# Two more early tiles of one gate, and the early gates loaded by another queue

## The chip, the core and the metric

The kernel runs on one core of a Trainium2 chip. The metric is the device time of one execution in microseconds (us), the lower the better. Three runs of the kernel before took 2232.28 to 2233.12 us, with a median of 2232.4. Engines are named as the profile names them: PE is TensorE (matmul), DVE is VectorE, ACT is ScalarE, POOL is GpSimd, SP is SyncE, which here only issues DMAs.

## What is computed

One step of a decoder layer for 1024 prompt tokens and 64 sample tokens together (1088 columns). Four token mixers (0: stick-breaking attention, 1: gated convolution, 2: RWKV-7, 3: spatial gating) each give a branch of 256 channels. What the change touches is their gated sum:

```
proj  = einsum('nlic,icd->nlid', br, w_branch)          # four branches, each 256 -> 1024
gates = sigmoid(x @ w_gate + b_gate).reshape(n, L, 4, 1024)
mix   = sum_i gates[i] * proj[i]
x     = LN1(alpha * x + mix @ w_o)                        # then memory cross-attention, then the MLP
```

Each gate i is 8 tiles of 128 channels by 1088 columns. One tile's gate is a product over 1024 inputs, its projection one over 256.

## The kernel before

All matrices are kept as a high and a low part of a 32-bit format, and each product is three matmuls (high by high, high by low, low by high). The 1088 columns are cut into three pieces of 384, 384 and 320, so a piece of a gate tile is 8 x 3 = 24 matmuls (tile `mm`) and a piece of its projection 2 x 3 = 6 (tile `pp`). A weight tile comes into a raw buffer `wraw`, ACT casts its high part `whi`, DVE subtracts the low part `wlo`; the projection's weights go the same way (`pwr`, `pwh`, `pwl`), a branch too (`braw`, `bhi`, `blo`). All these loads, of gates, projections, branches and of the folded memory weights, share a pool of two raw buffers.

The work runs in stages. First branch 2 (RWKV-7), then branches 3 and 0, which are long chains over all engines. Beside them a list of filler units (`fillers`, `groups`) gives PE matmuls at fixed points of the branches' code: projections of the inputs, branch 1, the memory's keys and values, and the early gates. `EARLY` says which gate tiles are made there: all 8 of gates 1 and 3, and the first tiles of gate 0. An early piece is computed into PSUM, copied by ACT (`gst`, L1268) and written to DRAM (`gate`, L1269, by SP). What is left in the list when branch 0 is done is drained at once (`self.fill(None)`).

Then comes the stage of the gates (`gates`, `add`). `LATE = (2, 0)`: gate 2 is computed here, 8 tiles by 3 pieces, so 24 steps. A step computes one piece of gate 2 and adds up to three pieces of an early gate (gate 1 beside tiles 0 to 3, gate 3 beside tiles 4 to 7), and a unit of the folded memory weights (`fst`, `fmh`). A tile of an early gate is loaded back whole (544 KB) into one of two buffers `add` (L1293, by SP), ACT takes its sigmoid in three pieces (L1311, `add<-add`), DVE multiplies by the projection (L1314) and POOL adds into `mix` (L1316). The piece computed in the step gets its sigmoid by ACT as `sg` (L1311, `sg<-mm`). The projections rotate over three PSUM buffers, so the fourth projection of a step needs DVE to have multiplied the first by `sg`. Last comes gate 0 with the same function: its early tiles are added one piece a step (`more`), tiles 6 and 7 are computed last, and `mix` goes to the output projection.

What order the instructions have on each engine is decided by a scheduler when the program is built, from its own estimate of durations; at run time each engine, and each queue of DMAs, takes its instructions strictly in that order. A DMA waits at its queue's head until its buffer is free, and what stands behind it waits too.

Of the kernel before, what the change touches and what calls it, by code (L numbers as in the profile page):

```python
# [24 lines left out]
CTEMPS = 8  # L25
ABUFS = 4

EARLY, LATE = ((1, 8), (3, 8), (0, 2)), (2, 0)
HALVES = (slice(0, 512), slice(512, 1024))
HR = (slice(0, 64), slice(64, 128))  # L30

# [19 lines left out]
class Kern:  # L51
# [1229 lines left out]
    def gates(self, w3):  # L1281
        nc, I = self.nc, self.I
        br, mix, begun = {}, {}, set()
        w0, br[LATE[0]] = self.first
        br[EARLY[0][0]] = self.load_br(self.bp[1], EARLY[0][0])
        ready = dict(EARLY)

        def add(i, m):

            early = m < ready.get(i, 0)  # L1290
            if early:
                gm = self.sp.tile([128, T], F32, name="add", tag="add", bufs=2)
                nc.sync.dma_start(gm, self.early[i][m])  # L1293
            else:
                w = w0 if i == LATE[0] and m == 0 else self.split_w(I["w_gate"][8 * i + m])
            p = self.branch_w(i, m)
            bh, bl = br[i]
            if m not in mix:
                mix[m] = self.g("mix", [128, T], self.xp)
            part = lambda a, kt: tuple(x[:, kt * 128:kt * 128 + 128] for x in a)  # L1300
            for c, (c0, n) in enumerate(CH):
                cs = slice(c0, c0 + n)
                if early:
                    src = sg = gm[:, cs]
                else:
                    ps = self.mm_ps()
                    self.gemm_b(ps, n, lambda kt: part(w, kt), lambda kt: (self.xhi[c][:, kt, :n], self.xlo[c][:, kt, :n]))
                    src, sg = ps[:, :n], self.sp.tile([128, 384], F32, name="sg", tag="sg", bufs=3)[:, :n]
                pp = self.wk_ps("pp")
                self.gemm_b(pp, n, lambda kt: part(p, kt), lambda kt: (bh[kt][:, cs], bl[kt][:, cs]), kts=2)  # L1310
                nc.scalar.activation(sg, src, AF.Sigmoid, bias=self.vec[:, 8 * i + m:8 * i + m + 1])  # L1311
                first = (m, c) not in begun
                begun.add((m, c))
                nc.vector.tensor_mul(mix[m][:, cs] if first else sg, sg, pp[:, :n])  # L1314
                if not first:
                    nc.gpsimd.tensor_add(mix[m][:, cs], mix[m][:, cs], sg)  # L1316
                yield

        def early(i):
            for m in range(ready.get(i, 0)):  # L1320
                yield from add(i, m)


        folded = self.folded(w3)
        for m in range(8):
            if m % 4 == 0:
                i = EARLY[m // 4][0]
                if m:
                    br[i] = self.load_br(self.bp[1], i)
                more = early(i)  # L1330
            for _ in add(LATE[0], m):
                for _ in range(3):
                    next(more, None)
                next(folded)
            next(folded)
        br[LATE[1]] = self.load_br(self.bp[1], LATE[1])
        more = early(LATE[1])
        for m in range(ready.get(LATE[1], 0), 6):
            for _ in add(LATE[1], m):
                next(more, None)  # L1340
        for _ in more:
            pass

        last = [add(LATE[1], m) for m in (6, 7)]
        act = None
        for c in range(3):
            for a in last:
                next(a)
            act = act or self.new_act()
            if c == 2:  # L1350
                self.wp, self.wi = [w3, w3, *self.wp], -1
                w = [self.split_w(I["w_o"][0, j]) for j in range(4)]
            self.split_mix(mix, act, c)
        return act, w
# [999 lines left out]
```

## Time and profile before

| | us |
|---|---|
| median of three runs | 2232.4 |
| the profiled execution | 2232.75 |
| its span, first to last instruction | 2231.0 |
| PE busy | 2146.9 (96%) |
| DVE busy | 1342.9 (60%) |
| ACT busy | 945.1 (42%) |
| POOL busy | 424.2 (19%) |

The stages on the span's clock: branches with fillers up to about 860 us (the last early gate piece is copied at 867), gate 2 with gates 1 and 3 from 867 to about 1092, gate 0 from there to about 1190, and the rest (output projection, cross-attention, MLP) to 2231. A row of the timeline has a start, a length, an engine, a line, the operation, and in brackets how long the engine was idle before it and what ended that. Matmuls overlap, so how fast they go is read from their starts, not from their lengths. The clock column is the clock that was granted to TensorE, 1.00 for 2.4 GHz.

### The profile page before, as it was taken

The numbers are of one execution on the slowest core, as the hardware profiler recorded it, in microseconds if no ns is written. First come the engines' busy times: TensorE is split into PE (matmuls) and PEld (weight loads), VectorE is DVE, ScalarE is ACT, GpSimd is POOL, SyncE is SP. The second block draws the span as 40 slices with busy tenths as digits, with TensorE's granted clock in tenths as the row PEclk, the third lists the DMA queues.
The fourth block names the chain that finished last, engine by engine and source line by source line (L and its number), as shares of the span: only waits on it lengthen the run. The fifth ranks groups of instructions, "written<-read, shape, count | busy, mean of one in ns | idle before, by whom it ended". The sixth has DMA issues, their size and how long they took to land.

```text
span 2231.0 us, 36111 instructions
## 1 busy us (share of the span) xinstructions
PE 2146.9 (96%) x13674; PEld 1918.4 (86%) x13674; DVE 1342.9 (60%) x2678; ACT 945.1 (42%) x1838; POOL 424.2 (19%) x482
## 2 busy tenths in 40 slices
PE   8998999999999999999999999999999999999998
PEld 8986777888989988998998877778999999788886
DVE  3365778755666674434324673479777776655477
ACT  4343343134555556444322362335444444544341
POOL 0111111012310310123220310000554543100000
PEclk9998999999999999999999999999999999999999
DMA  6322333145543435555324155733776677976552
GB/s 195 105 69 58 100 106 96 43 128 169 163 146 120 132 112 157 173 164 173 108 68 167 71 180 196 255 125 115 248 271 230 235 247 238 318 251 204 163 198 90
DMA packets 184838, 356.11 MB, mean 160 GB/s; under 512 B 36104, under 2 KB 92568, under 8 KB 184664
## 3 DMA queue, kind: packets, MB, share of 16 engines
q1 hardware_dynamic: 174216, 318.24, 43.7%
q0 software_dynamic: 10448, 35.57, 4.7%
q8 instruction: 107, 1.75, 0.3%
q14 instruction: 67, 0.55, 0.1%
HBM read 250.01 MB, written 103.73 MB: 159 GB/s over the span
## 4 chain that ended last, share of the span: by engine, by line
PE 74%; DVE 9%; DMA 9%; ACT 3%; issue 3%; POOL 1%; SPq 1%; DVEq 0%; ACTq 0%; POOLq 0%
PE mm L118 22%; PE m L118 14%; PE dn L2016 13%; PE mm L130 8%; PE sc L130 3%; PE pp L118 3%; DVE tpr L1014 1%; PE ds L2021 1%; PE gr L966 1%; DVE wlo L107 1%; DVE Ti L1015 1%; DMA vp<-in_vpages,pt 1%; DMA Li<-Ld 1%; PE wtp L503 1%; ACT whi L101 1%
## 5 line engine op out<-in xcount | busy, mean ns | idle before, releaser
L118 PE MATMUL mm<-ah,whi 128*128 128x384 f32 (+1 forms) x1176 | 395.8, 337 | 9.2 <-ACT ah L278 4.8
L118 PE MATMUL mm<-al,whi 128*128 128x384 f32 (+1 forms) x1176 | 392.7, 334 | 0.6 <-DVE al L279 0.6
L118 PE MATMUL mm<-ah,wlo 128*128 128x384 f32 (+1 forms) x1176 | 391.9, 333 | 0.6 <-DVE wlo L107 0.6
L2016 PE MATMUL dn<-dop 128*128 128x512 f32 x1344 | 317.9, 391 | 2.9 <-ACT dop L1691 2.9
L2016 PEld LDWEIGHTS dn<-dop 128*128 128x128 f32 x1344 | 253.0, 188 | 57.8 <-ACT dop L1691 3.3
L107 DVE TENSOR_TENSOR wlo<-wraw,whi 128x1024 fp32r<-128x1024 f32 (+2 forms) x145 | 158.9, 1104 | 173.0 <-ACT whi L101 170.1
L118 PEld LDWEIGHTS mm<-ah,whi 128*128 128x128 f32 x1176 | 224.5, 191 | 18.8 <-ACT ah L278 5.4
L118 PEld LDWEIGHTS mm<-al,whi 128*128 128x128 f32 x1176 | 224.3, 191 | 6.7 <-issue 3.5
L101 ACT CAST whi<-wraw 128x1024 fp32r<-128x1024 f32 (+1 forms) x130 | 132.9, 1027 | 228.3 <-PE mm L118 100.5
L118 PEld LDWEIGHTS mm<-ah,wlo 128*128 128x128 f32 x1176 | 224.3, 191 | 4.2 <-issue 1.9
L1692 DVE TENSOR_TENSOR dop<-wraw,dop 128x512 fp32r<-128x512 f32 x224 | 152.7, 713 | 109.2 <-ACT dop L1691 108.5
L118 PE MATMUL m<-xht,wo 128*128 128x272 f32 x1024 | 201.4, 292 | 5.3 <-DVE u L1894 3.2
L1691 ACT CAST dop<-wraw 128x512 fp32r<-128x512 f32 x224 | 133.0, 620 | 152.3 <-PE dn L2016 80.4
L130 PE MATMUL mm<-wlo,ah 128*128 128x512 f32 (+1 forms) x488 | 168.4, 349 | 3.7 <-DVE wlo L107 3.7
L130 PE MATMUL mm<-whi,ah 128*128 128x512 f32 (+1 forms) x488 | 169.1, 348 | 1.0 <-ACT stA L301 0.5
L118 PEld LDWEIGHTS m<-xht,wo 128*128 128x128 f32 x1024 | 164.8, 191 | 5.7 <-ACT u L1720 3.4
L130 PE MATMUL mm<-whi,al 128*128 128x512 f32 (+1 forms) x448 | 155.1, 346 | 0.0
L118 PE MATMUL m<-xh,wo 128*128 128x272 f32 x768 | 153.1, 293 | 0.0
L118 PE MATMUL m<-xlt,wo 128*128 128x272 f32 x512 | 149.1, 291 | 0.0
L118 PEld LDWEIGHTS m<-xh,wo 128*128 128x128 f32 x768 | 124.4, 191 | 0.0
L118 PE MATMUL m<-xl,wo 128*128 128x272 f32 x384 | 111.7, 291 | 0.0
L130 PEld LDWEIGHTS mm<-wlo,ah 128*128 128x128 f32 x488 | 92.4, 190 | 17.9 <-DVE wlo L107 4.8
(509 smaller groups left out, 4215.6 us busy)
## 6 DMA issues: line engine op xcount, KB each, us to landing
wraw<-hs SPq DMA_DIRECT2D x112, 256.0 KB, 4.1
wraw<-in_w_up SPq DMA_DIRECT2D x36, 512.0 KB, 4.6
wraw<-in_w_gate SPq DMA_DIRECT2D x32, 512.0 KB, 3.6
dw<-in_w_down SPq DMA_DIRECT2D x32, 512.0 KB, 4.9
hs<-sh SPq DMA_DIRECT2D x64, 256.0 KB, 2.6
wt<-dw SPq DMA_DIRECT2D x32, 512.0 KB, 3.4
wraw<-wt SPq DMA_DIRECT2D x64, 256.0 KB, 4.5
wraw<-in_w_down SPq DMA_DIRECT2D x48, 256.0 KB, 4.9
```

The lines of the kernel that those rows point to most:

```text
L101: nc.scalar.copy(hi[:, c], raw[:, c])
L107: nc.vector.tensor_sub(lo[:, c], raw[:, c], hi[:, c].bitcast(F32))
L118: nc.tensor.matmul(ps[:, :n], a, b, start=first and i == 0, stop=last and i == len(steps) - 1, skip_group_check=not first)
L130: nc.tensor.matmul(ps[:, :n], a, b, start=i == 0, stop=i == len(steps) - 1)
L503: self.nc.tensor.transpose(ps[:b.shape[-1], j * 128:j * 128 + 128], b, self.ident)
L966: nc.tensor.matmul(g[hh][:nb, j, :nb], p[HR[hh], pr, cs], q[HR[hh], pr, cs], start=True, stop=True)
L1014: nc.vector.tensor_mul(tv, Ti[:, 0:h, 0:t + 1], Li[:, 0:t + 1, t:t + 1].rearrange("p s o -> p o s").to_broadcast([128, h, t + 1]))
L1015: nc.vector.tensor_reduce(Ti[:, 0:h, t:t + 1], tv, axis=AX.X, op=ALU.add)
L1691: nc.scalar.copy(o[:, 0], src)
L1692: nc.vector.tensor_sub(o[:, 1], src, o[:, 0].bitcast(F32))
L2016: nc.tensor.matmul(ps[j], hs[:, a, c], w[:, b], start=first and k == 0, stop=last and k == 2, skip_group_check=n >= 16 and steps[n][0] in ...
L2021: nc.tensor.matmul(sp, rows[p][:, smp[i]].rearrange("p a n -> p (a n)"), ops[n][1][:, b], start=i != 2 and p == 0 and b == 0, stop=p == 15 ...
```

## The change

Three edits. `EARLY` gives gate 0 four early tiles, not two: six more pieces (24 matmuls each, a copy `gst`, a write to DRAM) join the end of the filler list, and their 144 matmuls leave the stage of gate 0. The load of every early tile (18 before, 20 now) is issued by POOL's queue, which has POOL's own instructions between, and no longer by SP's. And in the stage of gate 0, where now two tiles (4 and 5) and not four are computed before the last pair, two early pieces are added in each of six steps, not one in each of the first six of twelve.

```
-EARLY, LATE = ((1, 8), (3, 8), (0, 2)), (2, 0)
+EARLY, LATE = ((1, 8), (3, 8), (0, 4)), (2, 0)
...
             if early:
                 gm = self.sp.tile([128, T], F32, name="add", tag="add", bufs=2)
-                nc.sync.dma_start(gm, self.early[i][m])
+                nc.gpsimd.dma_start(gm, self.early[i][m])
...
         more = early(LATE[1])
         for m in range(ready.get(LATE[1], 0), 6):
             for _ in add(LATE[1], m):
                 next(more, None)
+                next(more, None)
```

The scheduler puts other rows around this. On PE the order is the same up to the end of branch 0 and in the stage of gate 2, and changes at the tail of branch 0 and in the stage of gate 0. On ACT it changes in the stage of gate 2 too.

ACT at the tail of branch 0, from the first sigmoid of an early gate. `e` and `z` are the attention's chain (L347 exponential, L348 logarithm, L355 exponential), whose two last `z` PE waits for; an ACT_TABLE_LOAD stands ahead of a function of another set. Before:

```order
L1268 COPY gst<-mm 128x384
L347 ACT_TABLE_LOAD
L347 ACTIVATE e<-e 128x512
L1247 CAST bhi<-braw 128x384
L348 ACT_TABLE_LOAD
L348 ACTIVATE e<-e,eps 128x512
L1247 CAST bhi<-braw 128x384
L1311 ACT_TABLE_LOAD
L1311 ACTIVATE add<-add,vec 128x384
L355 ACT_TABLE_LOAD
L355 ACTIVATE z<-z 128x512 x2
```

The same place now:

```order
L347 ACT_TABLE_LOAD
L347 ACTIVATE e<-e 128x512
L1311 ACT_TABLE_LOAD
L1311 ACTIVATE add<-add,vec 128x384
L355 ACT_TABLE_LOAD
L355 ACTIVATE z<-z 128x512
L348 ACT_TABLE_LOAD
L348 ACTIVATE e<-e,eps 128x512
L1268 COPY gst<-mm 128x320
L101 CAST whi<-wraw 128x1024
L1311 ACT_TABLE_LOAD
L1311 ACTIVATE add<-add,vec 128x320
```

The two casts of a branch and the second logarithm no longer stand ahead of the first of the two `z`. The second `z` comes after one more sigmoid, one more copy `gst` and one more table load, so between the two `z` there now stand a logarithm, two copies, a cast of weights, two sigmoids and three table loads. On PE, which transposes each `z` in four matmuls, 6 matmuls of a filler and not 14 now stand ahead of the first of these transposes, and 34 between the two groups of four, where 5 stood.

ACT in the stage of gate 2, at the first piece of tile 5 (tile 6's first piece has the same two orders). `add` is the sigmoid of the early tile of the next step, `sg` that of the piece which PE needs in this step. Before:

```order
L1233 COPY fst_10414<-mm_10407 128x512
L1219 CAST fmh_10517<-fraw_10515 128x512
L101 CAST whi_10510<-wraw_10509 128x1024
L1311 ACTIVATE add_10567<-add_10567,vec_76 128x384
L1311 ACTIVATE sg_10454<-mm_10429,vec_76 128x384
L1311 ACTIVATE add_10567<-add_10567,vec_76 128x384
L1311 ACTIVATE add_10567<-add_10567,vec_76 128x320
```

The same place now:

```order
L1233 COPY fst_10594<-mm_10587 128x512
L1219 CAST fmh_10697<-fraw_10695 128x512
L101 CAST whi_10690<-wraw_10689 128x1024
L1311 ACTIVATE add_10747<-add_10747,vec_76 128x384 x2
L1311 ACTIVATE add_10747<-add_10747,vec_76 128x320
L1311 ACTIVATE sg_10634<-mm_10609,vec_76 128x384
```

The `sg` stood behind one sigmoid of the loaded tile and stands behind three. In the second pieces of tiles 4 and 5 it stood ahead of all three and stands behind one; in the second piece of tile 6 it stood behind three and stands behind two.

ACT at the start of gate 0, where `whi` is the weight tile after the next. Before:

```order
L1258 CAST pwh<-pwr 128x256
L1311 ACTIVATE sg<-mm,vec 128x320
L1258 CAST pwh<-pwr 128x256
L101 CAST whi<-wraw 128x1024
L1233 COPY fst<-mm 128x512 x2
L1311 ACTIVATE sg<-mm,vec 128x384 x2
```

The same place now:

```order
L1258 CAST pwh<-pwr 128x256
L1233 COPY fst<-mm 128x512
L1311 ACTIVATE sg<-mm,vec 128x320
L1258 CAST pwh<-pwr 128x256
L1233 COPY fst<-mm 128x512 x2
L101 CAST whi<-wraw 128x1024
```

The copies that empty PSUM came behind the cast of a weight tile that has to be loaded first, and now come ahead of it. On POOL each load of an early tile stands right behind the addition that last reads the buffer.

## Rows read from the trace of the kernel before

**Rows 1.** The page, busy time, share of the span and instructions of each engine

```profile
PE 2146.9 (96%) x13674; PEld 1918.4 (86%) x13674; DVE 1342.9 (60%) x2678; ACT 945.1 (42%) x1838; POOL 424.2 (19%) x482
```

**Rows 2.** Windows: start:end, length, busy PE, PEld, DVE, ACT, POOL, clock, DMA, GB/s

```profile
840.00:880.00 40.00, 35.22 (x212) 31.99 (x210) 20.48 (x33) 27.20 (x43) 1.58 (x2) 0.91 0.45 137
...
985.00:1062.00 77.00, 72.57 (x403) 68.31 (x402) 32.79 (x49) 31.46 (x56) 30.89 (x32) 0.98 0.51 158
1062.00:1100.00 38.00, 35.22 (x188) 32.89 (x187) 12.29 (x18) 15.57 (x28) 4.64 (x5) 0.95 0.47 148
```

**Rows 3.** Waits of PE, 838 to 1110 us: total us, times, longest

```profile
PE pp L118 <- DVE sg L1314: 6.7, 6, 2.3
PE wtp L503 <- ACT z L355: 4.0, 1, 4.0
PE mm L118 <- ACT fst L1233: 2.7, 1, 2.7
```

**Rows 4.** Timeline of PE at the tail of branch 0

```profile
848.09 0.34 PE L118 MATMUL mm<-al,whi 128*128 128x384 f32 x1
852.41 1.11 PE L503 MATMUL wtp<-ident,z 128*128 128x128 f32 x4 [3.98 <-ACT z L355]
```

**Rows 5.** Timeline of ACT at the tail of branch 0

```profile
845.55 0.49 ACT L1247 CAST bhi<-braw 128x384 fp32r<-128x384 f32 x1
846.06 1.28 ACT L348 ACT_TABLE_LOAD   x1
847.36 0.72 ACT L348 ACTIVATE e<-e,eps 128x512 f32<-128x512 f32 x1
...
851.73 1.15 ACT L355 ACTIVATE z<-z 128x512 f32<-128x512 f32 x2
```

**Rows 6.** Timeline of PE at the start of gate 0

```profile
1093.47 0.69 PE L118 MATMUL mm<-ah,whi 128*128 128x384 f32 x1 [2.73 <-ACT fst L1233]
1094.27 0.52 PE L118 MATMUL mm<-ah,wlo 128*128 128x384 f32 x1
1094.59 0.52 PE L118 MATMUL mm<-ah,whi 128*128 128x384 f32 x1
```

**Rows 7.** Timeline of ACT at the start of gate 0

```profile
1091.89 1.04 ACT L101 CAST whi<-wraw 128x1024 fp32r<-128x1024 f32 x1 [2.02 <-DMA wraw<-in_w_gate]
1092.84 1.07 ACT L1233 COPY fst<-mm 128x512 f32<-128x512 f32 x2
```

**Rows 8.** The chain in order of time, in the stage of gate 0: start, length, what

```profile
1093.47 5.95 PE mm L118 x24
...
1101.52 4.16 PE mm L118 x24
```

**Rows 9.** Tile `add`, its loads by SP: duration ns min/median/max; landing us

```profile
L1293 SPq DMA_DIRECT2D add<-gate x18: 319/326/422, 833.6 to 1064.0; - x18
...
DMA to landing us min/median/max: 3.6/4.5/6.0
```

**Rows 10.** Tile `vp`, loads of 512 KB by POOL, gathered: ns; landing us

```profile
L507 POOL DMA_INDIRECT vp<-in_vpages,pt x8: 933/948/1777, 544.8 to 802.7; - x8
...
DMA to landing us min/median/max: 4.1/4.7/7.1
```

**Rows 11.** Timeline of POOL and of SP, one release of a buffer `add` and its load

```profile
1025.73 3.02 POOL L1316 TENSOR_TENSOR mix<-mix,add 128x384 f32<-128x384 f32 x3
...
1028.78 0.33 SPq L1293 DMA_DIRECT2D add<-gate  x1
```

**Rows 12.** Timeline of ACT in the stage of gate 2

```profile
992.27 0.58 ACT L1311 ACTIVATE sg<-mm,vec 128x384 f32<-128x384 f32 x1
...
1014.41 0.56 ACT L1311 ACTIVATE sg<-mm,vec 128x384 f32<-128x384 f32 x1
1014.88 1.06 ACT L1311 ACTIVATE add<-add,vec 128x384 f32<-128x384 f32 x2
```

**Rows 13.** Timeline of PE, a late projection in the stage of gate 2

```profile
1058.82 0.41 PE L118 MATMUL pp<-bhi,pwh 128*128 128x320 f32 x1 [2.29 <-DVE sg L1314]
```

More of the change, by code (lines that the diff above doesn't have):

```diff
@@ L26 @@
 ABUFS = 4
-EARLY, LATE = ((1, 8), (3, 8), (0, 2)), (2, 0)
+EARLY, LATE = ((1, 8), (3, 8), (0, 4)), (2, 0)
 HALVES = (slice(0, 512), slice(512, 1024))
@@ L1292, in add @@
                 gm = self.sp.tile([128, T], F32, name="add", tag="add", bufs=2)
-                nc.sync.dma_start(gm, self.early[i][m])
+                nc.gpsimd.dma_start(gm, self.early[i][m])
             else:
@@ L1339, in gates @@
             for _ in add(LATE[1], m):
+                next(more, None)
                 next(more, None)
```

## The prediction

> **What bounds the kernel now.** I read the shares of busy time first: PE is busy for 96% of the span [rows 1], so only what PE waits for, or how fast it is clocked, can move the time. The change leaves PE's count of matmuls alone: the 144 matmuls of two gate tiles go from the stage of gate 0 into the fillers. Then I read the windows around the places that the change touches [rows 2]: PE is idle for about 5 us of 40 at the tail of branch 0, for about 4 of 77 in the second half of gate 2, and for about 3 of 38 where gate 0 begins, and in each the clock's mean is under 1.00. So at most some 12 us and the clock's share are there to be won, on a base of 2232. Third, PE's waits in these stages [rows 3]: six waits for DVE's multiplication by `sg` (6.7 us), one for a `z` of ACT at the tail (4.0), one for a copy `fst` at the start of gate 0 (2.7). Each is priced below. A measurement of this kernel can tell about 0.2% from no change, that is 4.5 us.
>
> **The start of gate 0 (-4.5).** PE stands 2.73 us before the first matmul of this stage, for a PSUM buffer that `fst` empties [rows 6]. ACT was not busy then: it stood 2.02 us at the cast `whi` of a later weight tile, whose load had not landed, with the `fst` copies queued behind it [rows 7]. After the change the `fst` stand ahead of this cast, so the wait for a load is no longer passed on, and the 2.73 us should go. The clock adds to it: behind this wait the matmuls start 0.32 us apart [rows 6], and the 24 of this piece take 5.95 us, where a later 24 take 4.16 [rows 8]. They ran at the 1.2 GHz level after an idle stretch of PE; without it I take the 1.79 us back as well. Sum -2.73 - 1.79 = -4.5. What is late next: the same weight tile's cast, wanted one tile later by PE, with a tile's 3 x 24 matmuls (some 12 us by [rows 8]) as its cover; and the weights of the next early tile's projection, whose load and cast now come twice as fast in a step, since two pieces are added a step. I charge +0.3 for that (bounds 0 and +1.1, one cast of `whi` in [rows 7] whole on the path).
>
> **The tail of branch 0 (-1.0).** PE's last matmul before the wait starts at 848.09, and the transposes of `z` at 852.41 after 3.98 us of waiting [rows 4]. Ahead of that `z` on ACT stood two casts `bhi` (0.49 us the one shown), a table load (1.28) and a logarithm (0.72) [rows 5]: 2 x 0.49 + 1.28 + 0.72 = 2.98 us, which now come later. But PE also has only 6 matmuls of a filler ahead of this wait and not 14; at 4.16 / 24 = 0.173 us each [rows 8] these 8 covered 1.4 us. The first wait becomes 3.98 - 2.98 + 1.4 = 2.4, a gain of 1.6. Against it stands the second `z`: both came as one pair before (1.15 us for two [rows 5]), and now between them ACT has a logarithm (0.72), three table loads (3 x 1.28), a cast of weights (1.04 [rows 7]), two copies and two sigmoids (0.53 each, by the 1.06 for two in [rows 12]) and the `z` itself (0.58): 0.72 + 3.84 + 1.04 + 2.12 + 0.58 = 8.3 us. PE's 34 matmuls between them take 34 x 0.173 = 5.9 us, or 34 x 0.248 = 8.4 at the slower pace of [rows 8]. So a second wait of 0 to 2.4 us; I take 0.6, nearer to the slow end, because PE comes out of the first wait at whatever level that leaves. Sum -1.0, bounds -1.6 and +0.8. The 6 new pieces are matmuls like those around them; their copies and writes go on ACT and SP, which have idle time there (ACT 27 of 40 us busy [rows 2]), and cost nothing as long as nothing of the attention's chain stands behind them.
>
> **ACT's order in the stage of gate 2 (+2.5).** In the first pieces of tiles 5 and 6 the `sg` that PE needs for its fourth projection stands behind three sigmoids of an early tile, where it stood behind one: two more, 1.06 us [rows 12] each time, +2.1. In the second piece of tile 6 one fewer stands ahead: -0.5. In the second pieces of tiles 4 and 5 `sg` stood ahead of all of them (992.27 [rows 12]), and now stands behind one, and so behind the load of that tile; I take +0.5 each, one sigmoid (bounds 0, where the load has landed by then, and +1). Sum 2.1 - 0.5 + 1.0 = 2.6, taken as +2.5. From below the bound is -0.5: the first pieces may have slack for a microsecond, since the trace of before does not show PE waiting in every step (six times in 24 [rows 3]).
>
> **The queue of the loads (+0.8).** On SP an issue took 0.33 us and came right when POOL's last addition had freed the buffer (POOL's three began at 1025.73 and took 3.02, the load was issued at 1028.78) [rows 11]. So SP's queue was not what held these loads; the buffer was, and moving them to POOL's queue, where each stands right behind that addition, wins little at the issue. What can change is how long it takes to land: 4.5 us from SP in the median (3.6 to 6.0) [rows 9]. POOL loading such a tile is not in this trace; the nearest row is POOL's gather of 512 KB, 4.7 us (4.1 to 7.1), with 0.95 us of POOL at the issue [rows 10]. Four of PE's six waits for `sg` stand behind such a load, the longest 2.29 us [rows 13]; so a load that lands later is passed on there in full: 4 x 0.2 = +0.8. Bounds: 4 x (4.1 - 4.5) = -1.6 and 4 x (7.1 - 4.5) = +10.4. POOL's own time for 20 issues, 20 x 0.95 = 19 us, lies beside 424 us of POOL's work in 2231 [rows 1] and in the second half of gate 2 beside 46 idle of 77 us [rows 2]. SP is rid of 18 issues of 0.33 us, and what stood behind them no longer waits for a buffer of `add`: the loads of weights can go out earlier, but only two raw buffers take them, so I give that nothing here.
>
> The Trainium skill bears on this term. Its page "DMA: Bandwidth & Descriptors", section "Specifications", gives the first byte of a DMA about 1 us after issue on the GpSimd path and about 0.6 on that of SP and ACT. By that the term would be an estimate of 4 x 0.4 = +1.6 and the whole sum -1.1, or 2231.3; no run here shows a gate tile loaded by POOL yet, and the gather's row has 0.2 us. Its section "Issuing engines are not separate DMA queues" says that all issuers' DMAs run on the same 16 engines, so that another issuer saves only the time at the sequencer; the 0.33 us of the issue here agree that this is small.
>
> **The sum.** -4.5 + 0.3 - 1.0 + 2.5 + 0.8 = -1.9. The profiled execution took 2232.75 us, its span 2231.0; so 2230.85, and as the median of the runs is 0.35 below it, 2230.5.
>
> **The rivals.** *B, the full gain.* The reordered sigmoids hide in slack and the loads land sooner, because SP's queue no longer mixes them with weights: -4.5 at gate 0, -1.6 at the tail, -0.5 for the one `sg` that moved up, and the four waits behind a load shrink by the gather's best, 4 x (4.5 - 4.1) = 1.6 [rows 9, 10]: -8.2, or 2224.2. For it: the gather's 4.1 us is below 4.5, and SP, too, queues many waiting transfers. Against it: the load waits for the buffer, not for SP [rows 11].
>
> *C, slower.* POOL's loads land late. The place is the stage of gate 2, from tile 4 on, where the load is one step ahead of its use and ACT has `sg` behind it. If the median is 1 us or more above SP's 4.5, about nine steps that have no slack for it (the four that wait already, and the five whose `sg` the new order puts behind a sigmoid of the loaded tile or keeps there) pass on the 1 us each: +9, with -4.5 + 0.3 - 1.0 + 2.5 the sum is +6.3, or 2238.7. It decides for slower from a delay of about 0.8 us (9 x 0.8 - 2.7 = +4.5). For it: the gather's longest, 7.1 [rows 10], and a wait that also leaves PE at the lower clock level costs more than its length [rows 8]. Against it: the gather's median.
>
> *D, nothing comes of it.* The wait at the start of gate 0 comes back as a wait of the next tile's matmuls for the cast of the weights whose load was late by 2.02 us [rows 7], the clock falls there as it did, and the other terms cancel: 2232. Against it: 12 us of matmuls as a cover.
>
> **How the numbers follow.** The forecast 0.55, B 0.25, C 0.15, D 0.05. The forecast's own spread, some 2227 to 2235, lies mostly within 4.5 us of 2232.4: faster 0.12, same 0.40, slower 0.03. B is faster for 0.23 and same for 0.02; C slower for 0.13, same for 0.02; D same for 0.04, slower for 0.01. Together faster 0.35, same 0.48, slower 0.17. The range takes in B down to 2223 and C up to 2240 and leaves out what lies beyond either (both queue bounds whole, with the clock).
>
> **What would show it.** Right: PE's first matmul of gate 0 without a wait for `fst`, and its 24 in about 4.2 us; a wait for the first `z` of about 2.4 us and a second below 2.4; the waits for `sg` in the stage of gate 2 at some 8 to 11 us in place of 6.7; landings of `add` at about 4.7. Wrong: landings above 5.3 (C) or near 4.1 with waits for `sg` below 6 (B); a wait of PE for `whi` or `wlo` within the first two tiles of gate 0 (D); a gap of over 2.4 us at the second `z`, or new table loads of ACT on the path of the attention's chain, which would hit the tail's term.

## The result: slower, by the early tiles' loads

The changed kernel took 2246.43 us in the median of four runs (2242.96 to 2249.63), the kernel before 2232.34 beside it: 1.0064 times as long, 95% interval 1.0044 to 1.0085, some 14 us more. The forecast was 2230.5; the result lies above its range and beyond rival C's 2238.7, on C's side. The profiled execution's span was 2247.8 us.

On the page, the line that answers to [rows 1] has hardly changed: the engines do the same work.

```profile
PE 2145.1 (95%) x13674; PEld 1916.2 (85%) x13674; DVE 1341.3 (60%) x2678; ACT 950.2 (42%) x1846; POOL 440.3 (20%) x502
```

PE's waits in the stages that the change touches, 838 to 1130 us (what waited, for what: us in total, times, longest), answer to [rows 3]:

```profile
PE pp L118 <- DVE sg L1314: 24.8, 12, 4.7
PE wtp L503 <- ACT z L355: 2.5, 1, 2.5
PE mm L118 <- ACT sg L1311: 2.0, 2, 1.4
PE yps L447 <- DVE wT L434: 1.3, 1, 1.3
PE pp L118 <- DVE mix L1314: 0.6, 1, 0.6
```

The wait for `fst` at the start of gate 0 (2.7 before) is gone, the first wait for `z` is 2.5 where it was 4.0, and the waits for DVE's multiplication by `sg` went from 6.7 us in six to 24.8 in twelve. The windows (start:end, length, busy PE, PEld, DVE, ACT, POOL, clock, DMA, GB/s), of the tail, the two halves of gate 2, and gate 0, beside [rows 2]:

```profile
840.00:880.00 40.00, 36.17 (x239) 34.49 (x239) 13.74 (x18) 27.18 (x37) 0.55 (x1) 1.00 0.34 112
893.00:1004.00 111.00, 99.08 (x616) 96.86 (x615) 40.78 (x65) 43.81 (x78) 16.31 (x18) 0.97 0.49 153
1004.00:1118.00 114.00, 98.56 (x548) 92.20 (x548) 39.73 (x59) 42.15 (x74) 39.85 (x43) 0.96 0.46 142
1118.00:1215.00 97.00, 96.69 (x565) 93.77 (x564) 45.76 (x74) 38.58 (x75) 29.57 (x29) 1.00 0.35 109
```

The tail now keeps its clock (1.00, before 0.91) and gate 0 waits for next to nothing. All the loss is in the stage of gate 2: PE is idle there for 27 of 225 us and the clock is at 0.97 and 0.96. From the first projection to the last matmul of the folded weights this stage took 219.2 us before and now takes 244.8, 25.6 more. The other two stages got shorter. From the last group of `yps` (branch 0's last products) to the first projection there are 33.0 us, where there were 12.1, but six pieces more of 23.6 in all (twice 4.16 + 4.16 + 3.5) stand in them: 2.7 less. That group itself starts 0.8 later (859.87, before 859.07), which leaves 1.9. Gate 0, from that last matmul to the last projection, took 99.6 and takes 72.7: 26.9 less, of which 23.6 are those pieces, so 3.3 are won. Together -5.2, against +25.6. What comes behind gate 0, which the change does not touch, was 3.6 us shorter in this profile, and with it the sum is 16.8, the difference of the two spans.

One step of gate 2 shows how the loss comes about. The timeline of SP, POOL, ACT, DVE and PE in the changed kernel, gate 1's half; `mqT` is a weight tile of the folded memory weights, of which this step loads two:

```profile
920.05 1.99 SPq L100 DMA_DIRECT2D wraw<-in_w_mqT  x2
921.88 0.56 POOL L1293 DMA_DIRECT2D add<-gate  x1 [2.13 <-issue]
923.59 1.05 ACT L101 CAST whi<-wraw 128x1024 fp32r<-128x1024 f32 x1 [1.53 <-DMA wraw<-in_w_mqT]
...
929.83 1.05 ACT L101 CAST whi<-wraw 128x1024 fp32r<-128x1024 f32 x1 [4.19 <-DMA wraw<-in_w_mqT]
...
930.79 1.57 ACT L1311 ACTIVATE add<-add,vec 128x384 f32<-128x384 f32 x3
...
932.26 0.56 ACT L1311 ACTIVATE sg<-mm,vec 128x384 f32<-128x384 f32 x1
932.85 0.55 DVE L1314 TENSOR_TENSOR sg<-sg,pp 128x384 f32<-128x384 f32 x1 [0.72 <-ACT sg L1311]
...
933.46 0.41 PE L118 MATMUL pp<-bhi,pwh 128*128 128x320 f32 x1 [3.29 <-DVE sg L1314]
```

Both weight tiles and the early tile are in flight at once, the second weight tile reaches ACT at 929.83, some 8 us after its issue, and `sg`, which needs neither, stands behind its cast and behind three sigmoids of an early tile that is added only in the next step (in the kernel before these three stood ahead of that cast). In the other half, with the early tile alone late (POOL's issue, then ACT and PE):

```profile
1095.32 0.56 POOL L1293 DMA_DIRECT2D add<-gate  x1 [0.30 <-POOL mix L1316]
...
1102.25 1.12 ACT L1311 ACTIVATE add<-add,vec 128x384 f32<-128x384 f32 x2 [9.15 <-DMA add<-gate]
1103.28 0.56 ACT L1311 ACTIVATE sg<-mm,vec 128x384 f32<-128x384 f32 x1
...
1104.47 0.63 PE L118 MATMUL pp<-bhi,pwh 128*128 128x320 f32 x1 [4.74 <-DVE sg L1314]
```

I followed each of PE's waits for DVE and `sg` back to what ACT last waited for ahead of that `sg`. Before, 4.4 us were behind an early tile's load and 2.3 behind a weight tile; now 20.4 and 6.4. In gate 1's half these waits went from 2.3 to 11.4 us, in gate 3's half from 4.4 to 15.4.

### The profile page after: what moved, and what is told of

The parts are those of the page before. It is cut to its first block, busy times and chain, and to the rows that moved or that the text cites. A ratio compares the mean times of both kernels' runs of the same rounds, so it can differ in the third digit from the quotient of the medians.

```text
span 2247.8 us, 36135 instructions
## 1 busy us (share of the span) xinstructions
PE 2145.1 (95%) x13674; PEld 1916.2 (85%) x13674; DVE 1341.3 (60%) x2678; ACT 950.2 (42%) x1846; POOL 440.3 (20%) x502
```

## The experiments

Twelve kernels, each compared with the kernel before on the same chip. There the kernel before itself moved between 2215 and 2245 us from run to run, so the ratio with its interval is what counts; most intervals are some 0.4% wide, those of e1, e4 and e5 0.6 to 0.8%. "Of 2232" is that ratio times 2232 less 2232. The last column is the length of gate 2's stage, measured as above in the one profiled execution of each kernel. It shows what an edit does to this stage more clearly than the whole time does: what comes behind gate 0, which no edit touches, moved between 1033 and 1041 us from profile to profile.

| kernel | ratio | interval | us of 2232 | PE's waits for `sg`, us (times) | gate 2's stage, us |
|---|---|---|---|---|---|
| before | 1 | | 0 | 6.7 (6) | 219.2 |
| the change | 1.0064 | 1.0044 to 1.0085 | +14 | 24.8 (12) | 244.8 |
| e1, queue alone | 1.0088 | 1.0051 to 1.0125 | +20 | 20.7 (11) | 241.8 |
| e2, tiles alone | 0.9970 | 0.9948 to 0.9992 | -7 | 7.4 (6) | 219.4 |
| e3, `sg` first, POOL | 0.9964 | 0.9943 to 0.9985 | -8 | 2.0 (2) | 215.6 |
| e4, `sg` first, SP | 0.9925 | 0.9896 to 0.9953 | -17 | 1.8 (2) | 213.0 |
| e5, POOL, SP's order | 1.0100 | 1.0061 to 1.0139 | +22 | 20.6 (11) | 239.8 |
| e6, SP, POOL's order | 0.9977 | 0.9956 to 0.9998 | -5 | 10.9 (7) | 223.7 |
| e7, `sg` first, two tiles, SP | 0.9962 | 0.9941 to 0.9983 | -8 | 2.2 (2) | 215.5 |
| e8, one a step, SP | 0.9990 | 0.9968 to 1.0013 | -2 | 7.9 (6) | 219.7 |
| e9, SP, one issue later | 0.9986 | 0.9964 to 1.0009 | -3 | 9.8 (9) | 224.8 |
| e10, SP, three issues later | 1.0001 | 0.9981 to 1.0022 | 0 | 0.7 (1) | 226.3 |
| e11, weights on POOL too | 1.0047 | 1.0027 to 1.0068 | +10 | 17.5 (8) | 237.3 |
| e12, swapped | 1.0034 | 1.0020 to 1.0048 | +8 | 15.5 (11) | 233.0 |

**The change taken in two.** e1 is the kernel before with the queue changed; e2 the changed kernel with the queue changed back. PE's order is that of before in e1 and that of the changed kernel in e2.

```
e1, against before:   -  nc.sync.dma_start(gm, self.early[i][m])
                      +  nc.gpsimd.dma_start(gm, self.early[i][m])
e2, against the change:  the reverse
```

> The kernel before with the loads of the early gate tiles on POOL's queue and nothing else; PE's order is that of before. Theory Q (the queue: a load reaches ACT about 1 us later after its buffer is free, and the second weight tile of a step lands later beside it, so PE's waits for sg in the stage of gate 2 grow from 6.7 to some 25 us): 2244 to 2250 us, with these waits at 20 to 28 us. Theory T (the two tiles more and the two pieces a step cost the time): 2230 to 2235, waits for sg below 10.

> The changed kernel with the loads back on SP's queue: four early tiles of gate 0, two added a step; PE's order is that of the changed kernel. Theory Q: the stage of gate 2 is as before (waits for sg 5 to 9 us) and the start of gate 0 and the tail keep what they won in the changed kernel: 2225 to 2231 us. Theory T: 2242 to 2248.

Theory Q was met in both by the waits: e1 is 20 us slower, e2 7 us faster. The times in the median of the runs, 2250.13 and 2222.74 us beside 2230.85 for the kernel before, lie just outside what it gave. The two parts add up: the queue costs 20 us without the tiles and 21 with them (1.0064 against 0.9970), the tiles bring 7 and 5. In gate 2's stage the queue costs 22.6 and 25.4 us, the tiles nothing without the queue's change (219.4 against 219.2). PE's waits in e1 (the first four of the same view):

```profile
PE pp L118 <- DVE sg L1314: 20.7, 11, 3.4
PE wtp L503 <- ACT z L355: 4.0, 1, 4.0
PE mm L118 <- ACT fst L1233: 2.8, 2, 2.6
PE mm L118 <- ACT sg L1311: 1.9, 1, 1.9
```

and in e2:

```profile
PE pp L118 <- DVE sg L1314: 7.4, 6, 2.3
PE wtp L503 <- ACT z L355: 2.5, 1, 2.5
PE yps L447 <- DVE wT L434: 1.3, 1, 1.3
PE pp L118 <- DVE mix L1314: 1.0, 1, 1.0
PE mm L118 <- ACT fst L1233: 0.3, 1, 0.3
```

The `fst` and `z` waits go with the tiles, the `sg` waits with the queue. The same step as above in e2, with everything on SP's queue:

```profile
911.30 0.33 SPq L100 DMA_DIRECT2D wraw<-in_w_mqT  x1
912.86 0.33 SPq L1293 DMA_DIRECT2D add<-gate  x1
...
914.39 0.53 SPq L1234 DMA_DIRECT2D fold<-fst  x1
915.01 0.56 SPq L100 DMA_DIRECT2D wraw<-in_w_mqT  x1
917.84 1.58 ACT L1311 ACTIVATE add<-add,vec 128x384 f32<-128x384 f32 x3 [1.00 <-DMA add<-gate]
920.82 1.05 ACT L101 CAST whi<-wraw 128x1024 fp32r<-128x1024 f32 x1 [1.41 <-DMA wraw<-in_w_mqT]
921.78 0.58 ACT L1311 ACTIVATE sg<-mm,vec 128x384 f32<-128x384 f32 x1
...
923.65 0.42 PE L118 MATMUL pp<-bhi,pwh 128*128 128x320 f32 x1 [1.16 <-DVE sg L1314]
```

In SP's queue the second weight tile stands behind the early tile and a store of `fst`, and goes out 3.7 us after the first; the early tile is there after 5.0 us, the weight tile 5.8 after its issue, and PE waits 1.16 and not 3.29.

**`sg` ahead of the early pieces.** If PE waits because `sg` stands behind late loads on ACT, an order without that should free it though the loads stay late.

```
+  sa = nc.scalar.activation(sg, src, AF.Sigmoid, ...)
+  if not early:
+      self.sga = sa
+  elif i != LATE[1]:
+      self.behind(sa, self.sga)     # scheduled behind it, no wait
```

> The changed kernel, loads on POOL's queue, with one order fixed on ACT: in the stage of gate 2 the sigmoids of an early piece come behind the sigmoid sg of the step's own piece, never ahead of it. If the late loads cost time because sg stands behind them on ACT (theory Q, in its narrow form), the waits for sg fall from 25 us to below 8 though the loads land as late as in the changed kernel: 2222 to 2230 us. If it is the weight tile that lands late beside the loads (the cast whi ahead of sg), two or three waits of about 3 us stay, 2232 to 2240. Theory T: no change, 2242 to 2249.

> The same fixed order with the loads on SP's queue. Narrow form of theory Q: the load's landing no longer matters, so within 3 us of the run with POOL's queue, 2221 to 2228 us. If the weights beside the loads matter, it is 5 us or more below that run. Theory T: 2240 to 2246.

> The kernel before (two early tiles of gate 0, loads on SP's queue) with the fixed order of e4_sg_first_sp: sg ahead of the early pieces' sigmoids. If that order gains by itself, by the waits for sg (6.7 us) and by the sigmoids and table loads that leave the tail of branch 0 (the wait of 4.0 us there): 2219 to 2225 us, and the two tiles give e4_sg_first_sp another 5. If the order gains only where the loads are late: 2229 to 2233.

e3 keeps POOL's queue and is 22 us faster than the changed kernel (0.9964 against 1.0064). Its loads are issued as late as there, 0.30 to 0.53 us after the release. From issue to landing the trace tells only of three of its twenty loads, and of none in the changed kernel; these three are the min/median/max in the second line here:

```profile
L1293 POOL DMA_DIRECT2D add<-gate x20: 538/558/571, 835.2 to 1131.5; - x20
...
DMA to landing us min/median/max: 4.2/5.8/7.4
```

but PE waits for `sg` for 2.0 us in all:

```profile
PE pp L118 <- DVE sg L1318: 2.0, 2, 1.0
PE pp L118 <- DVE mix L1318: 1.9, 1, 1.9
PE mm L118 <- ACT sg L1311: 1.8, 1, 1.8
PE wtp L503 <- DVE wT L434: 0.9, 1, 0.9
```

So nearly all that the late loads cost, they cost through ACT's order: with `sg` first, gate 2's stage takes 215.6 us with POOL's loads, less than before. The expectation of waits that stay behind the weight tile's cast was wrong: in e3 that cast too waits 3.71 us for its load ahead of one `sg`, and PE then waits 1.04. e4 is the fastest of all, 2212.96 us in the median of its runs, and beats both kernels. That it is 0.4% below e3 was not expected by the narrow form (3 us); the two intervals overlap, and PE's waits for DVE and `sg` are as short in the one as in the other; a wait of 1.8 us for a buffer that `sg` empties, behind an early tile, is in e3 alone. Of the 4.3 us between the two profiled executions 2.6 lie in gate 2's stage and 3.2 behind gate 0, where both run the same code, so what the queue still costs stays open, some 3 us by the profiles. The same order without the two tiles (e7) brings 8 us, so it gains by itself, as expected, and adds to the tiles' 7. With it the early pieces' sigmoids, and with them all but one of the tail's loads of a table for a sigmoid, leave the tail of branch 0, where no wait for ACT's `z` is left (nor in e3 and e4).

**The order of the sigmoids, or the loads?** The scheduler gave ACT another order when the loads moved to POOL. e5 and e6 hold the sigmoids, and nothing else, in the other's order. That is the order of the sigmoids among themselves: where the casts of weights stand between them is left to the scheduler.

```
+  log["a" if early else "s"].append(sa)
...
+  seq = [log[k].pop(0) for k in ORDER]      # the order read from the other kernel
+  for a, b in zip(seq[1:], seq):
+      self.behind(a, b)
```

> The changed kernel, loads on POOL's queue, with the sigmoids on ACT held in the order that the scheduler gives them when the loads are on SP's queue (that of e2_tiles_alone); the order of every other instruction, on every engine, is that of the changed kernel. If the loads' own lateness costs the time (theory Q), little changes: 2241 to 2248 us, waits of PE for sg above 18 us, the difference to the changed kernel being the price of the order, some 2.5 by the prediction. If the new order of the sigmoids was what cost the time (theory O): 2223 to 2230, waits for sg below 10.

> The reverse: loads on SP's queue, with the sigmoids on ACT held in the order of the changed kernel. Theory Q: within 4 us of e2_tiles_alone, 2222 to 2230 us, waits for sg of 6 to 11 us. Theory O: 2238 to 2248, waits above 18 us.

This order is not what cost the time: e5 has SP's order and is no faster than the change (1.0100 against 1.0064, the intervals overlap), e6 has the change's order and is within 2 us of e2. In e6's profile the waits for `sg` are 3.5 us above e2's (10.9 and 7.4), and gate 2's stage is 4.3 us longer, which is about the +2.5 that the prediction gave the order. In the step shown above, e5 still has the cast of the second weight tile ahead of the three sigmoids, and e6 has it behind them; no run moves that alone.

**Two a step.** e8 is e2 with one `next(more, None)` in the stage of gate 0.

> e2_tiles_alone with one early piece added a step in the stage of gate 0, not two; the six that are left over are added behind the loop, with no gate matmuls beside them. If adding two a step costs nothing, as the prediction has it (0 to 1.1 us): within 2 us of e2_tiles_alone or slower than it by up to 5, since the six projections left over have only the loads to wait for. If two a step strains ACT or the loads: 3 us or more faster than e2_tiles_alone.

It is 0.2% slower than e2, intervals overlapping: adding two a step costs nothing that shows. In the profiles it gains: gate 0 takes 76.5 us in e8 and 72.7 in e2 and in the changed kernel. With one a step the `fst` at the start of gate 0 stands behind the cast of a weight tile again, as in the kernel before:

```profile
PE mm L118 <- ACT fst L1233: 2.2, 1, 2.2
```

**How late must a load be?** e9 and e10 leave the loads on SP and make them late by narrow loads of the same tile ahead of them.

```
+  for k in range(d):                # 1 in e9, 3 in e10
+      nc.sync.dma_start(gm[:, 8 * k:8 * k + 8], self.early[i][m, :, 8 * k:8 * k + 8])
-  nc.sync.dma_start(gm, self.early[i][m])
+  nc.sync.dma_start(gm[:, 8 * d:], self.early[i][m, :, 8 * d:])
```

> e2_tiles_alone (loads on SP's queue), with its order of sigmoids held, and one narrow load of 8 columns of the same tile issued ahead of each load in the stages of gate 2 and gate 0, so that the rest of the tile goes out one issue, 0.33 us, later. Theory L (lateness alone is enough: most of the loads have no slack behind them): 20 loads late by 0.33 us cost 3 to 6 us over e2_tiles_alone, 2226 to 2230 us. Theory W (a late load is passed on only in the four steps that waited before; the rest of the changed kernel's loss comes from weights that land late beside POOL's loads): 1 us, 2223 to 2225.

> The same with three narrow loads ahead, so 1.0 us later, about what the loads on POOL's queue lose between the buffer's release and ACT. Theory L: 12 to 20 us over e2_tiles_alone, 2236 to 2244 us, waits of PE for sg at 18 us or more. Theory W: 4 to 6 us over it, 2226 to 2230, waits for sg at 10 to 13 us.

e9 costs 4 us over e2 (5.4 in gate 2's stage), within theory L's 3 to 6, but the two intervals overlap. e10 costs 7: theory L, which wanted 12 to 20, missed, and theory W was a little below. But e10 is no clean test. Its loads were later than meant (the last part goes out 2.8 us after the release in the median, with other DMAs in between), and the scheduler planned around the longer load: on DVE the multiplication of an early piece now stands ahead of that by `sg` in several steps, and PE makes some projections earlier. So PE's waits for `sg` were 0.7 us, and 9.6 for a PSUM buffer that `sg` empties:

```profile
PE mm L119 <- ACT sg L1316: 9.6, 6, 4.5
PE wtp L504 <- ACT z L356: 2.5, 1, 2.5
PE pp L119 <- DVE add L1320: 1.6, 2, 0.9
```

e9 kept PE's order but for ten rows, and gives the size: in gate 1's half five of its loads reach ACT 4.1 to 4.8 us after the release (the other three went out 2.1 us after it, with other DMAs in between), and behind two of them, 4.6 us each, PE waits 0.63 and 0.25 us. The same two loads took 4.1 and 4.4 us before, without a wait; in the changed kernel none comes before 5.0 and there are waits of 1.3 to 1.7. What these two steps forgive ends about there, near 4.5 us.

**One queue or two?** e11 puts the weight tiles of these stages on POOL's queue too, so that one queue has everything again; e12 has only the weights there and the early tiles on SP's.

```
e11, against the change:  -  nc.sync.dma_start(raw[:, c], src[:, c])     # wraw
                          +  self.q.dma_start(raw[:, c], src[:, c])      # pwr alike; self.q is
                                                                         # nc.gpsimd in these stages
e12:  as e11, and         +  nc.sync.dma_start(gm, self.early[i][m])
```

> The changed kernel with the weight tiles of these stages (wraw, pwr) issued by POOL's queue as well, so that they stand in one queue with the early tiles again, as they did on SP's. If what costs the time is that two queues share the transfers and a weight tile no longer waits behind an early tile: back to 2224 to 2234 us. If POOL's queue is late by itself: no better than the changed kernel, 2245 us or more, since the weights become late too.

> The reverse of the change: the early tiles on SP's queue, the weight tiles of these stages (wraw, pwr) on POOL's; PE's order is that of e2_tiles_alone. Two queues still run side by side, but the early tile is on the one that was quick. If POOL's queue by itself makes a load late: early tiles reach ACT 4.8 us after their release as in e2_tiles_alone, PE's waits for sg behind early tiles stay below 6 us, and what is lost is lost by weights: 2226 to 2236 us. If it is the sharing of the transfers between two queues that makes them late: early tiles at 5.5 us or more, waits for sg behind them above 10 us, 2238 to 2248.

Neither came out whole. e11 is 10 us slower than before, so a single queue on POOL does not bring the time back; the waits behind weight tiles fell to 2.6 us (6.4 in the change), those behind early tiles only to 15.7 (20.4). In e12 the early tiles are on time though the weights run beside them on another queue: in gate 2's stage ACT has them 4.4 us after the release in the mean, 4.8 in e2, and 5.7 in e11. So in the mean it is not the sharing of the transfers between two queues that makes the tile late; POOL's queue does. (In the two steps that load two tiles of the folded weights beside it, the early tile took 5.8 and 7.0 us from its issue in e12, and 5.0 and 5.8 in e2: there the sharing shows.) Still PE waits 11.8 us behind early tiles, not below 6 as expected, and e12's time, +8 by its ratio, is that of the other theory. Some 10 of the 11.8 are in gate 3's half, and in the step shown there the release itself is late: POOL stands at its own DMA, which waits for a buffer, with the additions behind it that free the tile.

```profile
1028.11 0.56 POOL L1256 DMA_DIRECT2D pwr<-in_w_br  x1 [1.38 <-DVE wlo L108]
1028.70 2.81 POOL L1318 TENSOR_TENSOR mix<-mix,add 128x384 f32<-128x384 f32 x3
1031.54 0.32 SPq L1295 DMA_DIRECT2D add<-gate  x1
1035.78 0.61 ACT L1313 ACTIVATE add<-add,vec 128x384 f32<-128x384 f32 x1 [6.94 <-DMA add<-gate]
...
1037.44 0.41 PE L119 MATMUL pp<-bhi,pwh 128*128 128x320 f32 x1 [2.74 <-DVE sg L1316]
```

## Why the prediction was wrong, step by step

**The start of gate 0 (-4.5, +0.3): right in kind, a little large.** The wait for `fst` [rows 6] is gone, the stage gained 3.3 us. The first 24 matmuls start at 1138.05 and the projections behind them at 1142.32: 4.27 us, where they took 5.95 [rows 8]. Two pieces a step cost nothing; by the profile of e8 this gain even hangs on them, for with one a step gate 0 took 76.5 us, no less than the 99.6 of before without its 23.6.

**The tail (-1.0): right in kind, small.** The wait for the first `z` is 2.5 (2.4 was worked out); the second `z` brought no wait, but PE waited 1.3 for DVE's `wT`. Left out was the clock: 0.91 before in this window, 1.00 now, since the 3.98 us of idling [rows 4] are not there any more: before, it was granted 0.50 of full speed from 851.0 to 857.9. With it the tail gave 1.9, or 2.5 if counted from the table load ahead of the last exponential of L347 (843.72 before, 844.26 now) to the first projection; that is beyond the bound of -1.6.

**ACT's order (+2.5): about right.** e6 against e2 shows 3.5 us more of waits, 4.3 us more in gate 2's stage and 0.07% more time, e5 against the change no gain from the old order.

**The queue (+0.8): the step that failed.** Two things in it were wrong. First the lateness: 0.2 us were taken from the gather's row [rows 10]. Measured from the buffer's release to ACT's first sigmoid, over the loads for which ACT waited, it went from 4.7 us (14 loads) to 5.7 (16). Of that 1.0, 0.3 to 0.5 lie between release and issue: SP issued 0.03 us after it, POOL 0.30 after its own addition and 0.52 after DVE's multiplication. The prediction had seen that SP issues at the release [rows 11], and took for granted that POOL does. Here the Trainium skill's page "DMA: Bandwidth & Descriptors", section "Specifications", whose first-byte figures differ by 0.4 us between the two paths, pointed the right way; the 0.6 us of our total of 1.0 that lie behind the issue are nearer to it than the gather's row was. Second, and larger, how many steps pass it on. The prediction charged the four steps that waited before; there were twelve waits and two more for a buffer. `sg` stands behind an early tile's sigmoids in most steps, and most had hardly a microsecond of slack; rival C said so with nine steps and put the turning point at 0.8 us of delay. It was passed. For its place, tile 4 on, which is gate 3's half, C's +9 was near: PE's waits grew by 11.0 us there. But they grew by 9.1 in gate 1's half too, where neither the prediction nor C had a price. In all there are 20.4 us behind early tiles where it was 4.4, 6.4 behind weight tiles where it was 2.3, and the rest of the stage's 25.6 us with the clock, 0.96 and 0.97 after waits of up to 4.7 us.

**What no step had: the order that one queue keeps.** I wrote that the loads behind those on SP could go out earlier, and gave that nothing. They did, and it won nothing: in the step shown the second weight tile went out 1.7 us after the first, not 3.7, beside the early tile, and its cast began 9.8 us after the first's issue, where it was 9.5 in e2. What was lost is that the early tile was there first. In e2 it came 5.0 us after its issue, and its three sigmoids were done before that cast; in the changed kernel they ran behind it, 1.5 us more ahead of `sg`, and PE waited 3.3 and 3.2 us in the two such steps, where it waited 1.2 and 1.5 in e2. The changed kernel's trace does not tell when the early tile landed there; that of e5, where PE waits 3.4 and 3.5 us in these steps, has 8.2 and 8.3 us from its issue. The harm is not in the weight tile alone: in e3 ACT waits nearly as long for it (3.7 and 3.6 us, where it was 4.2 and 4.1), but `sg` comes right behind the cast, and PE waits 1.0 and 0.9.

**The chances.** 0.15 on C was too little: its mechanism needed one number, the lateness, that no row of before showed, and the bound that I had written down for it (7.1, +10.4) already stood above the 0.8 us at which it decides.

What stays open is how the 20 us of the queue divide between lateness, the lost order and the clock, and what makes a load of POOL late behind its issue. e9 and e10 could not make a load late with all else in its place, and e12 moves the weights' lateness as well. That the loss runs through ACT's order is shown, by e3.

## To carry to other kernels

Ask of a load not whether its data are late for their use, but what stands behind the first instruction that touches them: here the data were needed a step later, and an in-order engine made everybody wait for them at once. Putting the work that the busiest engine waits for ahead of such an instruction gained as much as the better queue did (22 us, e3, and 21, e2, both from the changed kernel), and some 8 to 10 us where the loads were on the better queue already (e7, e4). A queue that is shared also orders its transfers; when one kind of load moves away, the others go out beside it, and what came first may come last.

## What the runs showed of the hardware

- POOL's issue of a 544 KB load takes 0.56 us, SP's 0.33, and in the changed kernel it starts 0.30 us after POOL's own instruction and 0.52 after DVE's (0.30 or 0.53 after DVE's in e3), where SP, unless its queue holds something else first, starts 0.03 after either.
- In the stage of gate 0, where little else is loaded, POOL's loads were not slow once issued: 3.9 and 5.0 us to ACT's sigmoid in the changed kernel, 4.3 and 4.9 from SP in e2. They were later where weights were in flight too. In gate 1's half, over the loads for which ACT waited, they took 5.0 to 5.1 us in the mean (the changed kernel, e1, e5), SP's 4.3 (before, e2). In gate 3's half they took 5.7, 5.2 and 5.4, SP's 5.0 and 5.1: there the difference is not the same from kernel to kernel.
